# Expert dispatch, scaled copies: two early input loads issued from SyncE's queue instead of ScalarE's

## The chip, the cores and the metric

One core of a Trainium2 chip. The metric is the device time of one execution in microseconds (us). The engines that matter here are VectorE (DVE) and ScalarE (ACT), which multiply, SyncE (SP), which only issues transfers, and the core's 16 DMA engines, which move all data between device memory (HBM) and on-chip memory (SBUF). Transfers are issued by ScalarE and by SyncE; the trace shows ScalarE's as DMA queue q10 and SyncE's as q1.

## The reference

```python
batch, seq, hidden, n_experts = 16, 1024, 512, 8
k = 2
...
x_expanded = x[:, :, np.newaxis, :].repeat(k, axis=2)
weights = expert_weights[..., np.newaxis]
return (x_expanded * weights).astype(np.float32)
```

Each of 16,384 tokens has a row of 512 float32 values. The row is written twice, each time multiplied by one of the token's two weights. So 33.5 MB are read and 67.1 MB are written; expert_indices is not used.

## The kernel before

The tokens are cut into five groups of 24 x 128 and one of 8 x 128. Partition p of a group holds 24 (or 8) tokens that lie side by side in memory. A group of 24 is worked in two tiles of 12 tokens per partition, so there are eleven tiles, numbered 0 to 10: ten of 12 tokens and a last one of 8. A tile's load is 128 rows of 24 KB (3 MB), its store 128 rows of 48 KB (6 MB); for tile 10 it is 16 KB and 32 KB.

- `x_pool` has four input buffers (`XB = 4`), `o_pool` has two output buffers.
- Loads (`load`, line 79) are issued by ScalarE. Tiles 0 to 3 are issued ahead of everything (line 97), and tile i+4 after the work on tile i (line 128), when its buffer is free.
- Tile 0 is loaded in three pieces of 4 tokens per partition (rows of 8 KB, line 87), so that work can start on the first piece. Between the pieces goes the first group's weights (line 56, 128 rows of 192 bytes), and after the third piece the other weights (line 59, 512 rows of 192 bytes, and line 63, 128 rows of 64 bytes). Then follow the loads of tiles 1, 2 and 3.
- The products of a tile are 24 instructions of 128x512 (for tile 10: 16), two thirds on VectorE (line 115) and one third on ScalarE (line 109).
- When a tile's products are done, SyncE issues its store (line 124). Before the change SyncE issues nothing but the eleven stores.
- The compiled program hands eight completion semaphores to the transfers in turn. The ninth transfer in program order, the load of tile 3, takes the semaphore of the first one, and ScalarE waits for that one's completion before it issues the load.

A DMA queue takes its transfers in the order in which they were issued. All 16 DMA engines work for both queues; each engine carries 8 of the 128 rows of every transfer.

Of the kernel before, what the change touches and what calls it, by code (L numbers as in the profile page):

```python
# [1 line left out]

# [4 lines left out]


@with_exitstack
def kernel(  # L10
    ctx: ExitStack,
    tc: tile.TileContext,
    x: bass.AP,
    expert_indices: bass.AP,
    expert_weights: bass.AP,
    out: bass.AP,
):
    nc = tc.nc

    batch, seq, hidden = x.shape  # L20
    k = expert_weights.shape[-1]
    P = nc.NUM_PARTITIONS
    ntok = batch * seq
    assert ntok % P == 0
    A_TOTAL = ntok // P

    f32 = mybir.dt.float32
    row = k * hidden
    TX = 12
    TO = 12  # L30
    XB = 4

    groups = [[12, 12]] * 5 + [[8]]
    assert sum(sum(g) for g in groups) == A_TOTAL

    xf = x.rearrange("b s h -> (b s) h")
    of = out.rearrange("b s k h -> (b s) (k h)")
    wf = expert_weights.rearrange("b s k -> (b s) k")

    w_pool = ctx.enter_context(tc.tile_pool(name="w_pool", bufs=1))  # L40
    x_pool = ctx.enter_context(tc.tile_pool(name="x_pool", bufs=XB))
    o_pool = ctx.enter_context(tc.tile_pool(name="o_pool", bufs=2))

    w_tile = w_pool.tile([P, A_TOTAL * k], f32)

    def rows(of_all, done, T):
        return of_all[done * P : (done + T) * P, :].rearrange(
            "(p a) n -> p (a n)", a=T
        )

    T0 = sum(groups[0])
    G = len([g for g in groups[1:] if sum(g) == T0])
    head = (1 + G) * T0

    def first_weights():
        nc.scalar.dma_start(out=w_tile[:, : T0 * k], in_=rows(wf, 0, T0))  # L56

    def other_weights():
        nc.scalar.dma_start(  # L59
            out=w_tile[:, T0 * k : head * k].rearrange("p (g n) -> p g n", g=G),  # L60
            in_=wf[T0 * P : head * P, :].rearrange("(g p a) n -> p g (a n)", g=G, p=P),
        )
        nc.scalar.dma_start(  # L63
            out=w_tile[:, head * k :], in_=rows(wf, head, A_TOTAL - head)
        )

    tiles = []
    done = 0
    for group in groups:
        T = sum(group)  # L70
        a0 = 0
        for n in group:
            tiles.append((done, T, a0, n))
            a0 += n
        done += T

    loaded = []

    def load(i):
        if i >= len(tiles):  # L80
            return
        done, T, a0, n = tiles[i]
        x_tile = x_pool.tile([P, TX * hidden], f32)
        src = rows(xf, done, T)
        step = TX // 3 if i == 0 else n
        for at in range(0, n, step):
            nc.scalar.dma_start(  # L87
                out=x_tile[:, at * hidden : (at + step) * hidden],
                in_=src[:, (a0 + at) * hidden : (a0 + at + step) * hidden],
            )  # L90
            if i == 0 and at == 0:
                first_weights()
        if i == 0:
            other_weights()
        loaded.append(x_tile)

    for i in range(XB):
        load(i)
    for i, (done, T, a0, n) in enumerate(tiles):
        x_tile = loaded[i]  # L100
        outr = rows(of, done, T)
        for t in range(n):
            if t % TO == 0:
                o_tile = o_pool.tile([P, TO * row], f32)
            for kk in range(k):
                c = (done + a0 + t) * k + kk
                o = t % TO * row + kk * hidden
                if c % 3 == 2:
                    nc.scalar.mul(  # L109
                        out=o_tile[:, o : o + hidden],  # L110
                        in_=x_tile[:, t * hidden : (t + 1) * hidden],
                        mul=w_tile[:, c : c + 1],
                    )
                    continue
                nc.vector.tensor_scalar(  # L115
                    out=o_tile[:, o : o + hidden],
                    in0=x_tile[:, t * hidden : (t + 1) * hidden],
                    scalar1=w_tile[:, c : c + 1],
                    scalar2=None,
                    op0=mybir.AluOpType.mult,  # L120
                )
            if (t + 1) % TO == 0 or t + 1 == n:
                at = t // TO * TO
                nc.sync.dma_start(  # L124
                    out=outr[:, (a0 + at) * row : (a0 + t + 1) * row],
                    in_=o_tile[:, : (t + 1 - at) * row],
                )
        load(i + XB)

# [1 line left out]
_INS = ['x', 'expert_indices', 'expert_weights']  # L131
_OUTS = [((16, 1024, 2, 512), 'float32')]


# [23 lines left out]
```

## Time and profile before

| | |
|---|---|
| time, median of 3 runs | 241.15 us (240.93 to 243.14) |
| the profiled execution's own time | 241.01 us |
| its span, first to last instruction | 239.2 us |
| VectorE busy | 68.8 us (29%), 171 products of 482 ns |
| ScalarE busy | 54.7 us (23%), of it 85 products of 708 ns |
| moved by DMA | 33.69 MB read, 67.11 MB written, 421 GB/s over the span |
| issue to landing, load of 3 MB (median) | 80.3 us |
| issue to landing, store of 6 MB (median) | 31.4 us |

The page divides the span into 40 slices and gives the busy share of each in tenths. For the queues it counts packets: here a packet is one row of a transfer, and every transfer has 16 more of 4 bytes, which signal its completion. So the eleven stores are 11 x 144 = 1584 packets. "Landing" is the time from a transfer's issue to its last completion signal, and includes the time that it stood in its queue.

### The profile page before, as it was taken

Reading aid. Unit: us, or ns where it says so; the run is one execution under the profiler, and the core shown is the slowest. Engines: PE = TensorE matmul, PEld = TensorE weight load, DVE = VectorE, ACT = ScalarE, POOL = GpSimd, SP = SyncE. Lnnn points to the kernel's source line nnn. Section 1 sums busy time; section 2 is a strip of 40 time slices with the busy share of each in tenths; the row PEclk is TensorE's granted clock in tenths of the full one; section 3 lists DMA queues with packets and bytes.
Section 4 is the critical chain, followed back from the end, with each engine's and each line's share of the span. In section 5 each row is a group of like instructions: output and inputs, shape, how many; then the busy total and the mean of one; then the engine's idle time right before and its main releaser. Section 6 shows DMA issues by size and latency. Waiting matters only on the chain.

```text
span 239.2 us, 378 instructions
## 1 busy us (share of the span) xinstructions
DVE 68.8 (29%) x171; ACT 54.7 (23%) x86; POOL 0.2 (0%) x4
## 2 busy tenths in 40 slices
DVE  0911900450082019004500820280055009107000
ACT  0911700430080016004300800260052008005000
POOL 0000000000000000000000000000000000000000
DMA  7999999999999989989999999999989998999994
GB/s 256 427 374 411 452 419 444 460 394 440 415 527 394 452 375 423 510 362 444 427 427 501 419 394 460 394 493 427 444 362 436 448 481 370 507 394 411 451 438 192
DMA packets 4275, 100.82 MB, mean 421 GB/s; under 512 B 1200, under 2 KB 1200, under 8 KB 1200
## 3 DMA queue, kind: packets, MB, share of 16 engines
q1 hardware_dynamic: 1584, 67.11, 64.8%
q10 hardware_dynamic: 2688, 33.69, 33.7%
q14 instruction: 3, 0.02, 0.0%
HBM read 33.69 MB, written 67.11 MB: 421 GB/s over the span
## 4 chain that ended last, share of the span: by engine, by line
DMA 56%; another core or an unknown queue 19%; DVE 15%; ACTq 1%; issue 0%; DVEq 0%; SPq 0%
DMA out_dram<-o_tile 39%; DMA x_tile<-in_x_dram 17%; DVE o_tile L115 15%; ACTq L87 1%; ACTq L63 0%; ACTq L59 0%; ACTq L56 0%; DVEq L115 0%; DVEq L153 0%; SPq L124 0%
## 5 line engine op out<-in xcount | busy, mean ns | idle before, releaser
L115 DVE TENSOR_SCALAR o_tile<-x_tile,w_tile 128x512 f32<-128x512 f32 x171 | 68.8, 482 | 152.7 <-DMA x_tile<-in_x_dram 146.8
L109 ACT ACTIVATE o_tile<-x_tile,w_tile 128x512 f32<-128x512 f32 x85 | 53.4, 708 | 159.5 <-DMA x_tile<-in_x_dram 159.5
L109 ACT ACT_TABLE_LOAD x1 | 1.3, 1283 | 6.0 <-DMA x_tile<-in_x_dram 6.0
L142 POOL MEMSET const-bfloat16-1.0<- 128x1 bf16 x1 | 0.1, 102 | 0.0
L142 POOL MEMSET const-uint8-127<- 128x1 uint8 x1 | 0.1, 101 | 0.0
L142 POOL MEMSET const-float32-0.0<- 128x1 f32 x1 | 0.1, 99 | 0.2 <-issue 0.2
L142 POOL MEMSET const-float32-1.0<- 128x1 f32 x1 | 0.1, 98 | 0.0
## 6 DMA issues: line engine op xcount, KB each, us to landing
out_dram<-o_tile SPq DMA_DIRECT2D x10, 6144.0 KB, 31.4
x_tile<-in_x_dram ACTq DMA_DIRECT2D x9, 3072.0 KB, 80.3
out_dram<-o_tile SPq DMA_DIRECT2D x1, 4096.0 KB, 16.7
x_tile<-in_x_dram ACTq DMA_DIRECT2D x3, 1024.0 KB, 6.6
x_tile<-in_x_dram ACTq DMA_DIRECT2D x1, 2048.0 KB, 78.0
w_tile<-in_expert_weights_dram ACTq DMA_DIRECT2D x1, 96.0 KB, 8.6
w_tile<-in_expert_weights_dram ACTq DMA_DIRECT2D x1, 24.0 KB, 4.7
w_tile<-in_expert_weights_dram ACTq DMA_DIRECT2D x1, 8.0 KB, 8.3
```

What stands on the lines that cost most here:

```text
L87: nc.scalar.dma_start(out=x_tile[:, at * hidden : (at + step) * hidden], in_=src[:, (a0 + at) * hidden : (a0 + at + step) * hidden],)
L109: nc.scalar.mul(out=o_tile[:, o : o + hidden], in_=x_tile[:, t * hidden : (t + 1) * hidden], mul=w_tile[:, c : c + 1],)
L115: nc.vector.tensor_scalar(out=o_tile[:, o : o + hidden], in0=x_tile[:, t * hidden : (t + 1) * hidden], scalar1=w_tile[:, c : c + 1], scala ...
L142: nc = _bacc.Bacc("TRN2", target_bir_lowering=False, num_devices=1)
```

## The change

In `load`, the second piece of tile 0 and the whole of tile 1 are issued by SyncE instead of ScalarE. As SyncE issues in program order, both stand ahead of the first store in its queue. The third piece of tile 0, all weights and tiles 2 to 10 stay with ScalarE.

```diff
         for at in range(0, n, step):
-            nc.scalar.dma_start(
+            queue = nc.sync if i == 1 or i == 0 and at == step else nc.scalar
+            queue.dma_start(
                 out=x_tile[:, at * hidden : (at + step) * hidden],
                 in_=src[:, (a0 + at) * hidden : (a0 + at + step) * hidden],
             )
```

In the compiled program each queue then holds, in order:

```
ScalarE  tile 0 piece 1, first weights, tile 0 piece 3, other weights (2), tile 2, tile 3, then tiles 4 to 10
SyncE    tile 0 piece 2, tile 1, then stores 0 to 10
```

The products, their order on both engines and the stores are as they were. Tile 3's load still waits for the completion of tile 0's first piece.

## Prediction, made before the changed kernel ran

> **What bounds the kernel now.** First the page's head, its slices and its queue table, to see which resource is full:
>
> ```profile
> span 239.2 us, 378 instructions
> DMA  7999999999999989989999999999989998999994
> q1 hardware_dynamic: 1584, 67.11, 64.8%
> q10 hardware_dynamic: 2688, 33.69, 33.7%
> HBM read 33.69 MB, written 67.11 MB: 421 GB/s over the span
> ```
>
> The two queues' packets take 64.8 + 33.7 = 98.5% of the time of 16 DMA engines: 235.6 of 239.2 us. VectorE (29%) and ScalarE (23%) mostly wait, and the view of waits says for what:
>
> ```profile
> ACT o_tile L109 <- DMA x_tile<-in_x_dram: 159.5, 11, 17.1
> DVE o_tile L115 <- DMA x_tile<-in_x_dram: 146.8, 11, 15.7
> ```
>
> So an earlier input is worth nothing by itself. Only idle DMA time can be won or lost, and 239.2 - 235.6 = 3.6 us of it exists. The windows say where it lies (columns: stretch, length, busy us of VectorE, ScalarE and GpSimd, TensorE clock, DMA share, GB/s):
>
> ```profile
> 0.00:1.75 1.75, 0.00 (x0) 0.00 (x0) 0.20 (x4) 1.00 0.00 0
> 1.75:2.75 1.00, 0.00 (x0) 0.00 (x0) 0.00 (x0) 1.00 0.99 213
> 10.00:14.70 4.70, 2.42 (x6) 2.44 (x4) 0.00 (x0) 1.00 1.09 436
> 45.00:204.00 159.00, 51.17 (x128) 40.07 (x64) 0.00 (x0) 1.00 1.00 433
> 237.80:239.20 1.40, 0.00 (x0) 0.00 (x0) 0.00 (x0) 1.00 0.00 0
> ```
>
> No packet runs before 1.75 and none after 237.8: 1.75 + 1.4 = 3.15 of the 3.6 us. Loads alone (10 to 14.7) move at 436 GB/s, loads beside stores at 433, so the mix hardly sets the rate.
>
> Next, how the two queues share an engine. In a stretch with both at work, 25 to 30.45 us:
>
> ```profile
> q1 hardware_dynamic: 32, 1.57, 66.6%
> q10 hardware_dynamic: 32, 0.79, 33.5%
> ```
>
> Equal counts, two rows of each kind per engine: an engine alternates row by row. A 48 KB row takes 0.666 x 5.45 x 16 / 32 = 1.815 us, a 24 KB row 0.335 x 5.45 x 16 / 32 = 0.913; in proportion, an estimate, an 8 KB row takes 0.304. A load and a store side by side take 8 x (1.815 + 0.913) = 21.8 us, the kernel's period.
>
> Last, the timeline of the opening and of the end:
>
> ```profile
> 0.72 0.38 ACTq L87 DMA_DIRECT2D x_tile<-in_x_dram  x1
> 3.70 2.29 ACTq L87 DMA_DIRECT2D x_tile<-in_x_dram  x3
> 5.91 4.44 DVE L115 TENSOR_SCALAR o_tile<-x_tile,w_tile 128x512 f32<-128x512 f32 x11 [5.91 <-DMA w_tile<-in_expert_weights_dram]
> 10.88 2.07 DVE L115 TENSOR_SCALAR o_tile<-x_tile,w_tile 128x512 f32<-128x512 f32 x5 [0.53 <-DMA x_tile<-in_x_dram]
> 13.03 16.95 SPq L124 DMA_DIRECT2D out_dram<-o_tile  x2
> 23.14 6.42 DVE L115 TENSOR_SCALAR o_tile<-x_tile,w_tile 128x512 f32<-128x512 f32 x16 [10.18 <-DMA x_tile<-in_x_dram]
> ```
>
> ```profile
> 204.29 17.61 SPq L124 DMA_DIRECT2D out_dram<-o_tile  x2
> 217.06 4.45 DVE L115 TENSOR_SCALAR o_tile<-x_tile,w_tile 128x512 f32<-128x512 f32 x11 [12.84 <-DMA x_tile<-in_x_dram]
> ```
>
> Tile 0 is worked on from 5.91, store 0 goes out at 13.03, and tile 1 waits until 23.14. At the end tile 10 lands at 217.0 and its store is issued at about 221.6, while store 9 still runs: store 10 alone takes 8 x 1.213 = 9.7 us (row of 32 KB at two thirds of 1.815, an estimate), so store 9 ends near 237.8 - 9.7 = 228.1. Its last 6.5 us cover the last issue.
>
> **The change, part by part.**
>
> *Issues.* ScalarE loses two (369 ns median by the tile's view), SyncE gains two. The waits view shows SyncE held 0.7 us at the start, as ScalarE's first issue is (0.72), so its first goes out about then and its second 0.4 us later, some 11 us before its first store was due. Both sequencers then wait anyway: worth 0.
>
> The Trainium skill, "DMA: Bandwidth & Descriptors", section "Issuing engines are not separate DMA queues", speaks against the change: transfers of all issuers share the same 16 engines, so a second issuer only saves issue time. No row of this trace shows two queues of loads; by the rule the gain is at most those two issues, and the sum stays as it is.
>
> *Order in the queues*, per engine, row by row. Loads start at 1.75 and lose 0.47 us in the first microsecond (213 instead of 403 GB/s in the following window). From 2.2, piece 1 (ScalarE) and piece 2 (SyncE) alternate: 16 x 0.304 = 4.9, both done at 7.1. Before, piece 1 had this time to itself. Then the first weights, 8 tiny rows per engine, alternate with tile 1's 8 rows of 24 KB: 8 x 0.913 = 7.3, so they are done at about 14.4. Piece 3 follows alone, 8 x 0.304 = 2.4, to 16.8. With 0.7 us to land, an estimate (piece 1 landed 4.9 us after its issue, at 5.6; its rows end by 1.75 + 0.47 + 2.4 = 4.6, so it is 0.7 to 1), tile 0's products start at about 15 instead of 5.91 and end 4.44 + 2.07 = 6.5 us later. Store 0 is issued at about 21.6 instead of 13.03, 8.6 us late. As issue to first row took 1.7 us before (13.03 to the 14.7 at which the rows begin to mix), its rows start at about 23.3.
>
> The Trainium skill has another order: on the same page, section "Queues, rings and completion order", an engine drains a whole packet of about 9 to 17 descriptors of a queue before it changes to the next. By it the weights would not be held up by tile 1's rows one by one, and store 0 would be earlier; 32 against 32 in 5.45 us says that each turn is one row here. The sum is the same by both.
>
> *What the 8.6 us cost:* nothing, as long as loads cover them. All four first tiles, 12.6 MB, can be loaded without a store: 2.2 + 3 x 8 x 0.913 (tiles 1 to 3) + 24 x 0.304 (tile 0) = 31.4 us, against a first store row at 23.3. Cover left: 8.1 us. Without it each further microsecond would be one lost. Tile 3's issue waits for piece 1's landing, near 8 instead of 5.6; tile 2 fills the queue then, so 0.
>
> *Where the stall goes.* Tile 1 is already there when tile 0 is done, so store 1 follows 6.5 us behind store 0. Loads run ahead instead: tile 2 starts alone at 17.3 (other weights about 0.5), has 6 rows done by 23.3 and ends with store 0 beside it at about 29; tile 3 then ends at 29 + 21.8 = 51, against a landing at 66.7 before. Products are then held by the output buffers (two), not by inputs: tile 2 waits for store 0's landing, 23.3 + 21.8 + 0.7 = 46 (before, tile 2 began at 45.0). Store 2 is issued 6.5 us later, while store 1 runs to 67. From there the period is the same 21.8. Loads end about 15 us early, tile 10 near 202 instead of 217, and stores then run alone: store 8's rest, store 9 (14.5), store 10 (9.7). Tile 10's products wait for store 8; its 4.45 us and 2.4 for landing and issue fit under store 9's 14.5. No gap.
>
> *Sum.* Bytes and rows are unchanged: 235.6 us of DMA work; head 1.75, tail 1.4; outside the span 241.01 - 239.2 = 1.8. So 241.0, 0.1 under the median shown. Unknown: the opening with two queues, -0.5 to +0.5 (all of the first microsecond's 0.47 won back, or lost again); I take 0, since the engines wait there for first data either way. The end's unevenness (in 236 to 238 the DMA share was 0.04: a few engines finish late), from -0.45, which is all the idle time between the first and the last packet (3.6 - 3.15), to +1.0, half that window; taken as 0, as the last rows are the same stores.
>
> **Rivals.** *Two streams of loads hinder each other (slower).* Place: 2 to 23 us, where q1 and q10 both read, or one reads what the other did not. For: none of this was in the trace before, and at the joining of the second queue rows overlapped (a share of 1.12 in 14.7 to 23). Against: that stretch still moved 426 GB/s. Price: 21 us times the loss; it counts as slower from a loss of 11.5% (2.4 us). At 15% it is 3.2 us: 244.2. The far end, the 213 GB/s of the first microsecond throughout, would be 21 us.
>
> *Idle DMA time is won (faster).* Two issuers fill the opening and the end is even: 0.47 + 0.45 = 0.9, so 240.1. For more than 1% (2.4 us, about what a measurement can tell from no change) two thirds of all 3.6 us idle would have to go, and 3.15 lie before the first and after the last packet.
>
> *The order hardly changes.* If whole transfers take turns, weights pass at once and the opening looks much as before: 241.0 too, told apart only by the trace.
>
> **How the numbers follow.** Forecast 0.68, order hardly changed 0.10, hindrance 0.12, idle time won 0.10. Of hindrance 0.10 is beyond 1%; of idle time won 0.03. So faster 0.03, same 0.87, slower 0.10. The range joins the bounds: below, the 240.1 of the idle time won, less the 0.2 by which the lowest run lay under the median, so 239.9; above, 241.0 + 0.5 + 1.0 = 242.5. About 0.15 is left out.
>
> **What would show it.** VectorE's first product near 15, store 0 near 21.6, tiles 0 and 1 worked back to back; from tile 2 on products ended by stores, not loads; tile 10's load 15 us earlier against an unmoved end; the queues' shares again 98 to 99%. Wrong if a window before 30 us falls well under 420 GB/s, if a slice between the first and last is under 9 where none was, or if the last store starts after store 9 has ended.

## The result, and the profile after

The changed kernel takes 277.87 us (median of 6 runs, 277.39 to 278.49) against 241.06 us (240.91 to 243.14): a ratio of 1.152, 95% interval 1.149 to 1.155. It is slower by 15% where no change was forecast. The profiled execution took 277.55 us.

The page's head, slices and queue table:

```profile
span 275.8 us, 378 instructions
...
DMA  7999999999999999999999988985796289489891
...
q1 hardware_dynamic: 1872, 71.30, 63.6%
q10 hardware_dynamic: 2400, 29.49, 25.6%
...
HBM read 33.69 MB, written 67.11 MB: 366 GB/s over the span
```

The bytes are the same, and q1 has taken over what q10 gave up. But 63.6 + 25.6 = 89.2% of 275.8 us is 246.1 us of packets per engine, where before had 235.6: 10.5 us more work for the same rows. The other 29.7 us are idle, against 3.6 before: 26.1 us more. Together that is the 36.6 us by which the span grew. The slices show the idle time at the end, from about 170 us. The windows say the same (columns as above):

```profile
2.75:10.00 7.25, 0.00 (x0) 0.82 (x1) 0.00 (x0) 1.00 1.03 426
10.00:23.00 13.00, 6.66 (x17) 6.09 (x10) 0.00 (x0) 1.00 1.02 423
...
48.00:170.00 122.00, 32.12 (x80) 25.05 (x40) 0.00 (x0) 1.00 0.99 399
170.00:274.00 104.00, 23.72 (x59) 18.21 (x29) 0.00 (x0) 1.00 0.76 317
```

In the opening, up to 23 us, the rate is that of before. From 48 to 170 us the engines are as full as before (0.99), yet move 399 instead of 433 GB/s. After that a quarter of their time is idle. A full share with a low rate means rows that take longer. What the products wait for has changed too, from the inputs to the stores:

```profile
ACT o_tile L110 <- DMA out_dram<-o_tile: 183.0, 9, 24.4
DVE o_tile L116 <- DMA out_dram<-o_tile: 147.2, 8, 21.1
```

The timeline gives the opening and the period:

```profile
16.34 12.76 DVE L116 TENSOR_SCALAR o_tile<-x_tile,w_tile 128x512 f32<-128x512 f32 x32 [16.34 <-DMA w_tile<-in_expert_weights_dram]
22.85 91.06 SPq L125 DMA_DIRECT2D out_dram<-o_tile  x5
52.19 6.42 DVE L116 TENSOR_SCALAR o_tile<-x_tile,w_tile 128x512 f32<-128x512 f32 x16 [23.09 <-issue]
79.58 6.42 DVE L116 TENSOR_SCALAR o_tile<-x_tile,w_tile 128x512 f32<-128x512 f32 x16 [20.97 <-DMA out_dram<-o_tile]
107.09 6.42 DVE L116 TENSOR_SCALAR o_tile<-x_tile,w_tile 128x512 f32<-128x512 f32 x16 [21.08 <-DMA out_dram<-o_tile]
...
188.86 6.43 DVE L116 TENSOR_SCALAR o_tile<-x_tile,w_tile 128x512 f32<-128x512 f32 x16 [20.96 <-DMA out_dram<-o_tile]
...
214.75 6.42 DVE L116 TENSOR_SCALAR o_tile<-x_tile,w_tile 128x512 f32<-128x512 f32 x16 [19.46 <-DMA out_dram<-o_tile]
236.44 6.42 DVE L116 TENSOR_SCALAR o_tile<-x_tile,w_tile 128x512 f32<-128x512 f32 x16 [15.26 <-DMA out_dram<-o_tile]
```

Tiles 0 and 1 are worked back to back, as forecast. But from tile 2 (52.19) to tile 7 (188.86) a tile takes 27.3 us. In the kernel before, tiles 2 and 3 stand 21.9 us apart:

```profile
45.01 6.42 DVE L115 TENSOR_SCALAR o_tile<-x_tile,w_tile 128x512 f32<-128x512 f32 x16 [15.45 <-DMA x_tile<-in_x_dram]
66.87 6.42 DVE L115 TENSOR_SCALAR o_tile<-x_tile,w_tile 128x512 f32<-128x512 f32 x16 [15.44 <-DMA x_tile<-in_x_dram]
```

Only tile 9, with hardly anything left to load, follows tile 8 in 21.7 us.

**Which rows are longer.** The trace has one record for each packet, with its start and duration. The records do not name the engine. But in most of the trace packets follow each other on an engine without a gap, so the records can be strung together engine by engine; a few rows can't be placed, and the counts below are of those that can. Here are three of the 16 engines, from store 0's first rows on (L a load row, S a store row, then its duration in ns and its start in us; L9 and S9 are the completion signals, of 4 bytes):

```
a  L1072@26.09 S1815@27.16 L912@28.97 S1825@29.88 L912@31.70 S1815@32.61 L912@34.42 S1815@35.33 L912@37.14 S1815@38.05 L912@39.86 S1815@40.77 L912@42.58 S1815@43.49 L9@45.30 S1815@45.31 L912@47.12 S9@48.03 L912@48.03 S1815@48.94
b  S1834@26.35 L912@28.18 S1820@29.09 L912@30.91 S2676@31.81 L912@34.49 S2375@35.39 L912@37.77 S2482@38.67 L912@41.15 S2600@42.06 L912@44.66 S2202@45.57 L912@47.77 S2619@48.67 L9@51.29 S9@51.29 L912@51.30 S2201@52.21
c  S1815@26.69 L912@28.50 S1832@29.41 L912@31.24 S2531@32.15 L912@34.67 S2446@35.58 L912@38.02 S2588@38.93 L912@41.52 S2514@42.42 L912@44.93 S2081@45.84 L1241@47.92 S1944@49.16 L9@51.10 S9@51.10 L912@51.11 S2766@52.02
```

Twelve engines have store rows of 1.815 us, as before, and eleven of them look like a. Four look like b and c: from the third store row on theirs take 2.0 to 2.8 us. All load rows beside them stay at 0.912. What else differs between a and b is how the two transfers stand to each other. An engine carries a transfer in nine turns, 8 rows (numbered 0 to 7) and the signal (8). On b load signal and store signal follow each other: load row n always precedes store row n. On a the load's signal precedes store row 7: the load is one row ahead. Call the number of the load row less that of the store row behind it (counted round, modulo 9) the lead: 0 on b, 1 on a. The twelfth of the fast engines stands at lead 2; the expectations below count it with the eleven at lead 1.

Over the whole trace of before, all engines stand at lead 6, and of the 1,035 store rows directly behind a load row of known number none is over 1.9 us. After the change 159 of 179 rows at lead 0 are (mean 2.38 us), and 3 of 301 at lead 1. In all, 270 of the 1,280 rows of 48 KB are over 1.9 us, against 3 before, and these rows take 10.0 us more per engine: nearly all of the 10.5 us.

Four slow engines suffice to slow everything. A store is complete when the last engine is done, and the products wait for that with only two output buffers. Up to 110 us the rows at lead 0 take 2.43 us on average, so eight pairs of rows take 8 x (2.43 + 0.912) = 26.7 us, of the 27.3 measured. The twelve others finish their store rows sooner and go on with loads alone: from 26 to 170 us each of them carries 54 to 56 load rows, each of the four 42 or 43. Once no load is left in their queue they idle. That is the idle time after 170 us.

### The profile page after: what moved, and what is told of

Its sections match the earlier page's. It is cut to its first block, busy times and chain, and to the rows that moved or that the text cites. A ratio compares the mean times of both kernels' runs of the same rounds, so it can differ in the third digit from the quotient of the medians.

```text
span 275.8 us, 378 instructions
## 1 busy us (share of the span) xinstructions
DVE 68.6 (25%) x171; ACT 54.6 (20%) x86; POOL 0.2 (0%) x4
## 3 DMA queue, kind: packets, MB, share of 16 engines
q1 hardware_dynamic: 1872, 71.30, 63.6%
q10 hardware_dynamic: 2400, 29.49, 25.6%
## 4 chain that ended last, share of the span: by engine, by line
DMA 69%; DVE 14%; issue 9%; DVEq 0%; ACTq 0%; SPq 0%
DMA out_dram<-o_tile 63%; DVE o_tile L116 14%; DMA w_tile<-in_expert_weights_dram 5%; ACTq L88 0%; DVEq L154 0%; DVEq L116 0%; SPq L125 0%
```

## The experiments

Three theories at first. A: a store row is slow where the load row ahead of it has the same number (lead 0). B: an engine is slow where it stands apart from the other engines. C: the late store 0, or loads in SyncE's queue as such, upset the queues. For A an extra transfer of N rows is put between stores 0 and 1, on SyncE. It holds the stores back by N/16 + 1 turns on each engine (N/16 rows and a signal), so the lead grows by as much. In each such kernel `s_tile` is a new buffer of 128 x 2 float32, so the extra rows have 8 bytes; the extra transfer copies into it from store 1's tile and nothing reads it:

```diff
+                if i == 1 and t + 1 == n:
+                    nc.sync.dma_start(out=s_tile[:N, :], in_=o_tile[:N, TO * row - k :])
```

The medians of before in the three groups of runs were 240.79, 240.99 and 240.88 us.

**Before, with N = 32 (3 turns).**

> The kernel before, with one small extra transfer on SyncE's queue between store 0 and store 1: 32 rows of 8 bytes from the output tile into a spare tile, which is 2 rows and a signal, so 3 turns, on each engine. A transfer is 9 turns per engine (8 rows and a signal); call the lead of an engine the number of the load row less the number of the store row that follows it. In the trace before all 16 engines have lead -3 and 48 KB store rows of 1.815 us; in the changed kernel twelve have lead 1 (1.815 us) and four have lead 0 (2.0 to 2.7 us). The extra turns raise the lead by 3, so to 0 on all engines. Theory A (a store row is slow where it follows the load row of the same number): all 16 engines slow, period 8 x (2.4 + 0.91) = 26.5 us instead of 21.8 over 8 to 9 tiles, 241 + 38 to 42 = 279 to 285 us. Theory B (it is slow where engines stand at different leads): all engines stand alike, 241 us. Theory C (the late store 0 and loads that run ahead make products wait for stores): nothing is late here, 241 us.

Two runs, 256.09 and 261.87 us. In this execution twelve engines had started at lead 7 (that is, -2) and four at 6; three turns more brought the twelve to lead 1, where 1 of 222 store rows was slow, and the four to lead 0, where 44 of 50 were (mean 2.42 us). Up to the extra transfer the four were at 1.815. So before gets slow rows from a shift of its stores alone, without any load in SyncE's queue; tiles 2, 3 and 4 then began at 41.42, 67.09 and 94.73, so 25.7 and 27.6 us apart. The forecast that all 16 engines would reach lead 0 was wrong.

**After, with N = 16 (2 turns).**

> The changed kernel with the same extra transfer, of 16 rows: 1 row and a signal, 2 turns per engine, between store 0 and store 1. The leads go from 0 and 1 to 2 and 3. Theory A (row of the same number): only store 0's rows can still be slow on four engines, about 8 x 0.6 = 5 us on one tile, most of it hidden; 241 to 246 us. Theory B (engines at different leads): the difference between the engines stays, about 278 us. Theory C (store 0 late, loads ahead): both stay, about 278 us.

255.84 us, ratio 1.062 (1.044 to 1.080). Before the extra transfer's turns (26 to 50 us) 29 of 41 store rows at lead 0 were slow; after it (50 to 66 us) 1 of 39 at lead 2, on the same eight engines, and none of 30 at lead 3, on the other eight. One engine's rows read 2.60, 2.43, 2.46, 2.46, 2.36, 2.21 and then 1.815 six times. Later on, after 66 us, 46 of 192 rows at lead 2 were slow, and 22 of 240 at lead 3: these leads are not free of it, and the time missed the forecast of 241 to 246 us.

**Each half of the change alone.** Only tile 0's second piece on SyncE, tile 1 back on ScalarE:

```diff
-            queue = nc.sync if i == 1 or i == 0 and at == step else nc.scalar
+            queue = nc.sync if i == 0 and at == step else nc.scalar
```

> The changed kernel with tile 1's load back on ScalarE's queue, so SyncE issues only the second piece of tile 0 ahead of the stores. The first weights no longer share turns with 24 KB rows, so store 0 is issued near 13 to 14 us as before. Theory C (late store 0): 241 us. Theory A: 241 us unless the trace shows engines with lead 0, and then 270 to 285. Theory B: slow only if engines stand at different leads.

282.15 us, ratio 1.171 (1.167 to 1.176). Its timeline:

```profile
9.18 6.42 DVE L116 TENSOR_SCALAR o_tile<-x_tile,w_tile 128x512 f32<-128x512 f32 x16 [9.18 <-DMA w_tile<-in_expert_weights_dram]
15.69 37.24 SPq L125 DMA_DIRECT2D out_dram<-o_tile  x3
19.18 6.43 DVE L116 TENSOR_SCALAR o_tile<-x_tile,w_tile 128x512 f32<-128x512 f32 x16 [3.58 <-DMA x_tile<-in_x_dram]
```

Store 0 goes out at 15.69, 2.7 us later than in before and 7.2 us earlier than in after, and the kernel is slower than both. So how late store 0 is does not decide. As before with N = 32 has slow rows with no load in SyncE's queue, C falls. At lead 0, 154 of 165 store rows are slow; at lead 1, 5 of 355.

Only tile 1 on SyncE:

```diff
-            queue = nc.sync if i == 1 or i == 0 and at == step else nc.scalar
+            queue = nc.sync if i == 1 else nc.scalar
```

> The changed kernel with the second piece back on ScalarE's queue, so SyncE issues only tile 1's load ahead of the stores. Tile 1's 24 KB rows now take turns with piece 1 and all that follows it, so store 0 is issued at about 17 to 22 us. Theory C (late store 0, loads ahead): slow, 265 to 278 us. Theory A: slow only if the trace shows engines with lead 0, and 241 us otherwise. Theory B: slow only if engines stand at different leads.

Two runs far apart, 278.38 (the profiled one) and 250.86 us, so the time gives no verdict and may depend on how the engines happen to come to stand; only one of the two has a trace. In the profiled one 134 of 147 rows at lead 0 are slow (mean 2.44 us), and 7 of 311 at lead 7.

**Other distances.** Before with N = 16 (2 turns), and before with N = 48 (4 turns):

> The kernel before with the small extra transfer of 16 rows, 2 turns per engine, between stores 0 and 1. With 3 turns (r1_before_lead0) twelve engines came to lead 1 and four to lead 0, and only the four were slow; they had stood at -2 and -3. With 2 turns the same start gives twelve engines at lead 0 and four at -1. Theory A (a store row is slow where it follows the load row of the same number): twelve engines slow, or none where all 16 start at -3 and come to -1; 255 to 285 us in the first case, 241 in the second. Theory B (the engines that stand apart from the others are slow): the four are slow and the twelve not, 255 to 262 us, or 241 if all stand alike.

> The same with 48 rows, 4 turns: from -3 and -2 to leads 1 and 2. Theory A: no engine at lead 0, 241 to 243 us. Theory B: if the engines stand at two leads, four are slow again, about 255 to 260 us.

N = 16: 257.11 us, ratio 1.066 (1.060 to 1.072). Here 13 engines had started at lead 6 and three at 7. The 13 came to lead 8, with 8 slow rows of 273, six of them on one engine; the three came to lead 0 and had 42 of 48 slow. N = 48: 249.05 us, ratio 1.033 (1.030 to 1.036). All 16 engines went to lead 1, and 3 of 320 rows were slow; none came to lead 0. Its windows and its queue table from 30 to 105 us show a kernel at full rate:

```profile
30.00:105.00 75.00, 19.28 (x48) 15.04 (x24) 0.00 (x0) 1.00 1.01 434
```

```profile
q1 hardware_dynamic: 542, 21.14, 65.3%
q10 hardware_dynamic: 526, 11.40, 35.5%
```

21.14 MB are 430 rows of 48 KB, and 0.653 x 75 x 16 / 430 = 1.822 us each. So its 8 us over before are not those of slow rows in this stretch. A wait stands out: store 4's products are done at 88.11 + 6.43 = 94.54, and its issue is at 107.17 (timeline).

```profile
88.11 6.43 DVE L118 TENSOR_SCALAR o_tile<-x_tile,w_tile 128x512 f32<-128x512 f32 x16 [17.62 <-DMA out_dram<-o_tile]
...
107.17 0.33 SPq L129 DMA_DIRECT2D out_dram<-o_tile  x1
```

The eight completion semaphores go to the transfers in turn, and one transfer more shifts the rotation: store 4 now takes the semaphore that tile 5's load, issued at 29.62, still holds, and waits for it. The store queue runs dry, and from 111 us on the engines stand at several leads (2 to 6). Packets take 1.5 us more per engine than in before, idle time 6.7 us more. That the wait makes the 8 us was not tried by itself. The same wait holds store 4 back in before with N = 32 (products done at 101.15, issue at 120.25) and N = 16 (101.95 and 121.55), so their times are not those of slow rows alone. An extra transfer is no clean tool after its first periods: the rows and the engines within one run are the evidence, not the times.

After with N = 64 (5 turns):

> The changed kernel with 64 rows, 5 turns, between stores 0 and 1: leads 0 and 1 become 5 and 6 (6 is the lead of all engines in the kernel before, counted modulo 9). Theory A: slow rows only in store 0, then 1.815 us everywhere, 241 to 245 us. Theory B: four engines stay apart, 255 to 278 us. With 2 turns it was 255.8.

253.43 us, ratio 1.051 (1.044 to 1.058), where 241 to 245 was expected. Ahead of the extra transfer 13 of 16 rows at lead 0 were slow; behind it 1 of 432 at lead 6, where most engines then stood, and 28 of 97 at lead 5, 7 of 27 at lead 7 on the few others. Tile 3 began 28.1 us after tile 2, and the next four tiles 23.1 to 23.7 us apart, against 21.8.

**Same number, or standing apart?** In nearly all of these the slow engines were also the few (in after with N = 16 they were eight of 16). N = 112 (8 turns) in after should exchange the two: the many go from lead 1 to 0, the few from 0 to 8.

> The changed kernel with the extra transfer of 112 rows, 8 turns per engine, between stores 0 and 1: leads 1 (twelve engines) and 0 (four) become 9, which is 0 again, and 8. It asks whether lead 0 is slow also where most engines have it. Theory A (a store row is slow where it follows the load row of the same number): after store 0 about three quarters of the store rows beside 24 KB rows take over 1.9 us instead of a quarter, and the four that were slow run at 1.815 us. Theory B (only engines that stand apart are slow): a quarter or fewer, the twelve stay at 1.815 us. The time is 270 to 290 us by A, as the slowest engines set the period either way, and 250 to 278 us by B.

266.64 us, ratio 1.107 (1.097 to 1.117). From 26 to 48 us four engines at lead 0 had 15 of 21 rows slow, eleven at lead 1 none of 77. From 80 to 150 us the eleven stood at lead 0, and 188 of 188 rows were slow (mean 2.49 us); the four, at lead 8, had none of 79. The sixteenth went from lead 2 to 1 and had 3 of 20. One engine of the eleven (d) and one of the four (e):

```
d  S2379@78.05 L912@80.43 S2389@81.33 L912@83.72 S2475@84.63 L912@87.10 S2534@88.01 L912@90.54 S2488@91.45
e  S1815@78.79 L912@80.61 S9@81.51 L9@81.52 S1815@81.53 L912@83.34 S1815@84.25 L912@86.06 S1815@86.97 L912@88.78 S1815@89.69
```

The queue table from 80 to 110 us:

```profile
q1 hardware_dynamic: 171, 7.42, 70.7%
q10 hardware_dynamic: 174, 3.78, 29.3%
```

151 rows of 48 KB, 0.707 x 30 x 16 / 151 = 2.25 us on average over fast and slow engines. The majority is slow now, and B falls. An engine's slowness goes with its lead.

**What about the row is it?** First, the load's addresses in HBM. In after, tiles 0 to 9 are read from the tokens of the next partition, so each load row lies elsewhere (the products are those of other tokens):

```diff
         src = rows(xf, done, T)
+        if T == T0:
+            src = xf[done * P + T : (done + T) * P + T, :].rearrange("(p a) n -> p (a n)", a=T)
```

> The changed kernel, but tiles 0 to 9 are loaded from one partition row further on in memory: partition p gets the tokens of partition p+1, so the output of these tiles is that of other tokens. SBUF addresses, rows, turns and bytes are as in the changed kernel. If the slow pairing is one of memory addresses (load row k and store row k at related addresses in HBM), it moves by a row: the slow engines are then at lead -1 and those at lead 0 run at 1.815 us. If it is one of SBUF partitions, or one of the DMA engine's own turns, it stays at lead 0 and the time stays at 270 to 285 us.

279.14 us, ratio 1.158 (1.154 to 1.161), and 123 of 132 rows at lead 0 slow: this shift of a row's address in HBM makes no difference. Second, the partitions. A load row n and a store row n of one engine have the same SBUF partition, if every transfer's rows are dealt to the engines in the same way; no trace here names a row's partition. If loads and stores are cut into two halves of 64 partitions, an engine's turns can pair the same partitions, or, with the stores' halves exchanged, other ones.

```diff
+            for h in (0, 64) if i > 1 else (None,):
+                ps = slice(None) if h is None else slice(h, h + 64)
...
+                for h in (0, 64):
...
```

In the second kernel the stores' loop runs over `(64, 0)`.

> The changed kernel with the loads of tiles 2 to 10 and all stores cut into two transfers of 64 partitions, partitions 0 to 63 first on both sides: 2 x 5 turns per tile and engine on both queues. Control for the next. Theory A in both forms: engines where load row k comes ahead of store row k again have store rows of 2.2 to 2.7 us; 255 to 285 us. There are more transfers, so more waits on completions too; the rows decide, not the time alone.

> The same, but stores take partitions 64 to 127 first, loads 0 to 63 first. Load row k and store row k of equal turn then belong to partitions 64 apart. If the slow pairing is one of SBUF partitions (a row read from the partition that the row before it wrote), engines at lead 0 (modulo 10) run at 1.815 us and those at lead 5 are slow. If it is one of turns (equal numbers in the two queues), engines at lead 0 are slow as in the control.

The control alone took 363.38 us, ratio 1.509 (1.500 to 1.517), the crossed one 354.55 and 363.74 us. In the control's page, slices and queue table:

```profile
DMA  8999999999999999999999999999999999999951
...
q1 hardware_dynamic: 2048, 71.30, 69.8%
q10 hardware_dynamic: 2544, 29.49, 26.5%
```

The engines are full, with 96.3% of 362.4 us where 235.6 us did. Load rows too grew, to 0.9 to 1.9 us for most (3.5 at most), and store rows took 1.8 to 5 us. Cutting the transfers in half brought a larger loss of its own, in which the question drowned. Whether it is the same partition or the same turn that hinders stays open.

**Without two queues.** All loads from tile 1 on are issued by SyncE too, so loads and stores stand in one queue:

```diff
-            queue = nc.sync if i == 1 or i == 0 and at == step else nc.scalar
+            queue = nc.sync if i > 0 or at == step else nc.scalar
```

> The changed kernel with all loads from tile 1 on issued by SyncE too, so that loads and stores stand in one queue and an engine never alternates between rows of two queues after the opening; only tile 0's pieces 1 and 3 and the weights are ScalarE's. Theory A (and B): no slow rows, 1.815 us throughout; all bytes move at the full rate and a load still stands in the queue behind every store: 240 to 244 us. If the slow rows came from products that wait for stores, or from the late store 0, they would stay: 265 to 280 us.

244.16 us, ratio 1.014 (1.010 to 1.017). Slices and queue table of its page, and a line of its timeline:

```profile
DMA  6999999899999999999999999899989999999991
...
q1 hardware_dynamic: 3168, 98.57, 95.0%
q10 hardware_dynamic: 1104, 2.23, 2.4%
```

```profile
67.03 12.76 DVE L116 TENSOR_SCALAR o_tile<-x_tile,w_tile 128x512 f32<-128x512 f32 x32 [32.77 <-DMA w_tile<-in_expert_weights_dram]
```

2 of 1,280 rows of 48 KB are over 1.9 us, and packets take 236.4 us per engine, as good as before's. This kernel has two loads in SyncE's queue ahead of the stores just as after has, and far later products (tile 2 waits until 67.03 for the other weights, whose tiny rows alternate with whole rows of the full queue). It loses only 1.4%, and has no slow rows: no load row of another queue stands between its store rows. The loss of after therefore belongs to the alternation of the two queues, not to the place of the two loads. No kernel tried here beats before.

The rows by lead, over the kernels (rows over 1.9 us, of how many):

| lead | slow rows |
|---|---|
| 0 | after 159 of 179; others 44 of 50, 29 of 41, 154 of 165, 134 of 147, 42 of 48, 123 of 132, 188 of 188 |
| 1 | after 3 of 301; others 1 of 222, 5 of 355, 3 of 320, 1 of 243, 0 of 77 |
| 2 | 1 of 39 at first, 46 of 192 later |
| 3 | 0 of 30 at first, 22 of 240 later |
| 5 | 28 of 97, on a few engines |
| 6 | before 0 of 1,035; 1 of 432 |
| 7 | 7 of 311; 7 of 27, on few engines |
| 8 | after 3 of 70; 8 of 273, 0 of 79 |

## Why the prediction was wrong

- *Issues: worth 0.* Right. SyncE's first issue is at 0.73, and nothing waits for it.
- *Order in the queues, row by row.* Right, and the rows strung together above show it directly: one row of each queue in turn. Products were forecast for about 15 and began at 16.34, store 0's issue for 21.6 and came at 22.85, its first rows for 23.3 and came between 26.3 and 28.9, engine by engine. So the opening was 1.3 us later than worked out, and the first rows 3.0 to 5.6 us. Beside the late opening, a reading of the trace before was wrong: 1.7 us from issue to first row (13.03 to 14.7). The rows from 14.7 on are load rows that run long, 0.9 to 2.0 us; the first store row starts at 17.72, 4.7 us after the issue. After the change it was 3.5 to 6.0 us, engine by engine.
- *The 8.6 us are covered by loads.* Right: from 10 to 23 us the engines move 423 GB/s. The first rows of store 0 lie well before 31.4, where the cover would have ended.
- *Loads run ahead, and products are ended by stores.* Right in kind: eight of VectorE's waits now end with a store. But tile 10's last load row ended at 234.0, not near 202.
- *"From there the period is the same 21.8."* This is the step that failed, and with it the sum's "Bytes and rows are unchanged: 235.6 us of DMA work" and "No gap". It took 1.815 us as the price of a store row whatever stands ahead of it. It had been measured at one lead only, 6, as all of before runs at it. At lead 0 it is 2.4 us, the period 27.3, packets take 246.1 us, and 29.7 us are idle instead of 3.6, as twelve engines wait for four. Tile 2 started 6.2 us later than the 46 forecast (3.0 of it from the first row), five periods of 27.3 add 5 x 5.5 = 27.7, and tile 8 still 4.1 (25.9 instead of 21.8): 38.0 late at tile 8, of which the span's end, 36.6 late, wins back 1.4.
- *Where the engines came to stand* was probably set by when the first rows started. By the prediction's schedule store 0 would have met tile 2 with six rows done, near before's lead. With 4.7 us from issue to first row the same schedule has tile 2 done at 24.6 and tile 3 one or two rows in at 26.3, and the trace has store 0 meet the start of tile 3, at leads 0, 1 and 2. So a new lead could have been forecast from the trace before; its price could not, as nothing there ran at lead 0. That the start of the first rows set the lead is read from the schedules, not tried; that the lead makes the rows slow, given the alternation, was.
- *The sum's terms.* As listed they give 240.6, not 241.0; the 0.45 us idle between first and last packet is left out of the list. Beside a miss of 36.8 us this is nothing.
- *Rival "two streams of loads hinder each other".* It had the right sign and the wrong place. Its stretch from 2 to 23 us moved 423 to 426 GB/s, so two streams of loads cost nothing here. What hindered was a load beside a store, which the prediction had taken off the list with 433 against 436 GB/s, again measured at lead 6 alone.
- *"Idle DMA time is won", "the order hardly changes".* Neither: idle time grew by 26.1 us, and the order changed as worked out.

The rule from the Trainium skill, "DMA: Bandwidth & Descriptors", section "Issuing engines are not separate DMA queues", that a second issuer only saves issue time, held for the gain. It does not bound the loss: here two queues side by side cost 36.8 us at one lead and nothing at another.

What stays open is why equal numbers hinder. The HBM row of the load was shifted without effect; SBUF partition against turn was not settled. Nor is it shown why lead 0 becomes slow only at the third to fifth row, and why leads 2, 3, 5 and 7 are slow in part.

## What to carry to other kernels

A row price read from a trace holds for the order of rows in that trace; a change that moves a store's start against the loads' can change the price without changing a byte. When two queues alternate on full engines, compare the rate at full share (here 399 against 433 GB/s), then the durations row by row and engine by engine, as four slow engines of 16 set the period through the completion. If the order of loads and stores cannot be fixed, one queue for both gave up 1.4% here and removed the effect.

## What the runs showed of the hardware that was not expected

- A store row of 48 KB behind a load row of the same number on the same engine takes 2.0 to 2.8 us instead of 1.815; the load row itself stays at 0.912. It sets in after two to four rows and goes with the lead at once.
- The 16 engines came to stand at different leads, eleven, four and one in after, twelve and four or 13 and three in runs of before with an extra transfer, though the program treats all alike.
- One small transfer more shifted the rotation of the completion semaphores so that a store ready at 94.54 was issued at 107.17.
- Loads and stores cut into two halves of 64 partitions kept the engines full at 278 GB/s, and took 363 us.
